# Branch gates through DRAM, attention spread to the end of the gate products, and the written order kept there

## The chip, the core and the metric

The kernel runs on one core of a Trainium2 chip. The core has a matrix engine (PE, with its weight loads shown apart as PEld), a vector engine (DVE), a scalar engine (ACT), a general engine (POOL), and a sync engine (SP) that here only issues transfers. Each engine takes the instructions of its own queue in order, and semaphores make one wait for another. The time is that of one execution on the device in microseconds; a kernel is run several times, and the median counts.

## What is computed

One step of a hybrid layer for 320 tokens, 256 of a new stream and 64 of a running one, model width 2048, all in float32. Cut to what matters:

```python
xn, u, v, q, k, va = _project(xp, norm_mix_g, w_in)        # rmsnorm, one product, gelu on u and v
q, k = _partial_rope(q, pos_p), _partial_rope(k, pos_p)    # 16 of 64 head columns are rotated
vn = _layernorm(v, gmlp_ln_g, gmlp_ln_b)
a = _gmlp_mix(u, vn, gmlp_ws, gmlp_bs)                     # mixes within chunks of 128 tokens
o = _swa_prompt(q, k, va, attn_sinks)                      # 32 heads, 4 key heads, sliding window, sink
g = sigmoid(xn @ w_gate + b_gate); g_a, g_b = halves(g)
x = x + (g_a * (a @ w_branch_a) + g_b * (o @ w_branch_b)) @ w_out
h = _rmsnorm(x, norm_ffn_g)
y = _rmsnorm(x + (silu(h @ w_ffn_gate) * (h @ w_ffn_up)) @ w_ffn_down, final_norm_g)
```

The outputs are y and the new keys, values and normalised v rows.

## The kernel before

**Products.** Activations lie transposed, features on the partitions, tokens on the free axis (T = 320). Each operand is split into a high part `hi` of the type that PE multiplies and the remainder `lo`, and a product takes three matmuls: hi by x-high, hi by x-low, lo by x-high (L168 to L170). A *group* makes 512 output columns: `gemm` (L152) takes four PSUM banks and goes through eight blocks of two row tiles of the weights, 24 matmuls a block, 192 a group. The groups come in the order that `products` lists: first the keys and values (kv, in `first_gemm`), then `QV` (four groups of queries q0 to q3, one for each key head with its eight heads, mixed with four groups of v), then the gates of branch B (gb0 to gb3), w_branch_b (bb), u, the gates of branch A (ga), w_branch_a (ba), w_out and the feed-forward groups.

**Weights.** SP fetches each block of 512 KB into one of four `raw` buffers, four blocks before it is split (`fetch`, L127). ACT writes `hi` (L135) and DVE `lo` (L144), two blocks before their matmuls, into three buffers each. In `gemm`, a block issues `hi` of the block after next, half its matmuls, then `lo` and a fetch, then the rest.

**The calendar.** After every 12 matmuls `gemm` calls `pump()`, which advances a slot counter and issues what `later(slots, fn)` has entered for that slot. There are 16 slots to a group. Small work is hung between the products in this way. Slots are counted here from the end of kv: q0 is slots 1 to 16 and so on to slot 128, the gb groups are slots 129 to 192, bb begins after slot 192.

**Attention.** A group q_g ends in `q_done` (L639): ACT copies the four banks to `qr`; a slot later ACT issues four transfers that bring the partner rows for the rotation to `swp` (`rope_swap`, L365); in slots 5 and 7 after the group `rope_turn` (L370) rotates two tiles each with three DVE operations (times cosine, partner times sine into a scratch tile of the pool tag `st`, sum; L375 to L377). Then ACT and DVE split the queries into high and low (`hi`, `lo` of `q_parts`, L508 and L512), in the five slots before `QK0[g]`. From slot `QK0[g]` after the group, five *units* follow, one for each set of 64 query positions, `5 * n` slots apart (L654). A unit's steps stand in `attend` (L516 to L637), each with its slot: scores on PE (0), peak on DVE (1), exponentials on ACT (2), weights on DVE and ACT (3, 4), pack, a DVE transpose (5), spread, four SP transfers to a DRAM tile `pd` (6), gather, one or two SP transfers back to `pf` (8), part high on ACT (11) and part low on DVE (12), values on PE (14), lower on ACT (15), total on DVE (16). The total puts the unit's output into `f1`. Units of positions 2 to 4 have 192 keys, in a block of 128 and one of 64. 

**v.** A group v_g ends in `v_done` (L659): DVE multiplies by the norm factor, ACT applies the gelu (slot 1), PE transposes (3 to 6), DVE and ACT copy to `tok` (L676, L677), DVE takes statistics (9).

**After QV.** `at = 19` (L748): from 17 slots after the last v group the pool `attn` is closed and the pool `late` opened in its place, the attention's output is split from `f1` into `yh`, `yl` (`split_o`), v is normalised (`v_aggr`, `v_load`, `v_norm`, L728 to L730) and the mixing weights are loaded and turned (`load_ws`, `turn_ws`). This falls into the gb groups. A gb group ends in `sigmoid` (L762): DVE multiplies by the norm factor, ACT applies the sigmoid. The gates of gb0 stay in a tile of tag `st`, those of gb1 to gb3 go to `f1`, whose rows the split has read by then. `flush()` (L778) empties the calendar before bb, and bb multiplies its products with the gates into `f1` (L784).

**Order.** Within `tc.manual_schedule()` each engine gets its instructions as the program writes them. Before, this holds from the start to the end of kv (`startup`, L94 and L487) and for the tail (L941). Between them the tile framework's planner orders the queue of every engine, by its own estimate of durations, from the dependencies and the written order. PSUM has eight banks under one tag: four belong to the current group, the others to scores (two), values, transposes, and to the next group.

Of the kernel before, what the change touches and what calls it, by code (L numbers as in the profile page):

```python
# [10 lines left out]
F32 = mybir.dt.float32  # L11
F32R = mybir.dt.float32r
AF = mybir.ActivationFunctionType
ALU = mybir.AluOpType
# [4 lines left out]
P = 128  # L19
D = 2048  # L20
DC = D // P
T = 320
# [3 lines left out]
W = 512  # L26
# [8 lines left out]
    [(0, 4), (512, 4), (1024, 4), (1536, 4)],  # L35
    [(0, 4), (512, 4), (1024, 4), (1536, 2), (1792, 2)],
]
QV = [("q", 0), ("q", 1), ("v", 0), ("q", 2), ("v", 1), ("q", 3), ("v", 2), ("v", 3)]
QK0 = [14, 24, 18, 12]

NK = [64, 128, 192, 192, 192]
KC = [0, 0, 0, 64, 256]
# [28 lines left out]
def tile_hybrid_step(ctx: ExitStack, tc: tile.TileContext, a: dict, outs: list):  # L71
    nc = tc.nc
    y_p, y_s, ko_p, vo_p, ko_s, vo_s, gv_s = outs
    w_in, w_gate = a["w_in"][0], a["w_gate"][0]
# [5 lines left out]
    tmp = ctx.enter_context(tc.tile_pool(name="tmp", bufs=2))  # L80
    psum = ctx.enter_context(tc.tile_pool(name="psum", bufs=8, space=PSUM))
    dram = ctx.enter_context(tc.tile_pool(name="dram", bufs=1, space=DRAM))
# [8 lines left out]
    def later(slots, fn):  # L91
        calendar.setdefault(now[0] + max(1, slots), []).append(fn)

    startup = tc.manual_schedule()  # L94
    startup.__enter__()

    def pump():
        now[0] += 1
# [3 lines left out]
    def flush():  # L102
        while calendar:
            pump()
# [262 lines left out]
            nc.scalar.dma_start(swp[b : b + 8, 0:nt, :], qr[b + 8 : b + 16, 0:nt, :])  # L367
            nc.scalar.dma_start(swp[b + 8 : b + 16, 0:nt, :], qr[b : b + 8, 0:nt, :])

    def rope_turn(t0):  # L370
        t1 = tmp.tile([P, 2, T], F32, tag="st", name="rope_t1")
        cb = cos_t.unsqueeze(1).broadcast_to([P, 2, T])
        sb = sin_t.unsqueeze(1).broadcast_to([P, 2, T])
        q2 = qr[:, t0 : t0 + 2, :]
        nc.vector.tensor_tensor(q2, q2, cb, op=ALU.mult)  # L375
        nc.vector.tensor_tensor(t1, swp[:, t0 : t0 + 2, :], sb, op=ALU.mult)
        nc.vector.tensor_tensor(q2, q2, t1, op=ALU.add)  # L377

    ka = ap.tile([P, 4, NPOS], F32R, name="ka")
    kl = ap.tile([P, 4, NPOS], F32R, name="kl")  # L380
# [103 lines left out]
        return [p[:, :T] for p in ps]  # L484

    ps = first_gemm()
    startup.__exit__(None, None, None)  # L487
    for t in range(4):
        nc.scalar.activation(qr[:, t, :], ps[t], AF.Copy)
    later(1, lambda: rope_swap(2))  # L490
# [1 line left out]
    for i, n in xs:  # L492
        later(7 + i, lambda i=i, n=n: new_v(i, i * P, n))
        later(9 + 2 * i, lambda i=i: v_blocks(i))
    later(8, lambda: rope_turn(0))
    later(11, k_out)
    later(11, rope_scale)
    for g in range(4):
# [17 lines left out]
    def attend(g, n, qs, st):  # L516
# [72 lines left out]
        def part(low):  # L589
            if not low:  # L590
                st["mm"] = []
            for i, (blk, kn) in enumerate(VB[n]):
                src = st["pf"][:kn, i, :]
                l = vv[:, blk, g, :]
                if kn == P:
                    if not low:
                        st["ph"] = ap.tile([P, 512], F32R, tag="ph", name=f"ph_{g}_{n}")
                        nc.scalar.activation(st["ph"], src, AF.Copy)
                    else:
                        pl = ap.tile([P, 512], F32R, tag="pl", name=f"pl_{g}_{n}")  # L600
                        nc.vector.tensor_tensor(pl, src, f32(st["ph"]), op=ALU.subtract)
                        st["mm"] += [(l, st["ph"]), (l, pl)]
                else:
                    if not low:
                        st["p2"] = ap.tile([P, 512], F32R, tag="p2", name=f"p2_{g}_{n}")
                        nc.scalar.activation(st["p2"][0:64], src, AF.Copy)
                    else:
                        p2 = st["p2"]
                        nc.vector.tensor_tensor(p2[64:128], src, f32(p2[0:64]), op=ALU.subtract)
                        st["mm"] += [(l, p2)]  # L610
# [11 lines left out]
        def total():  # L622
# [9 lines left out]

        return (
            (0, scores), (1, peak), (2, power), (3, lambda: weigh((1, 3))), (4, lambda: weigh((0, 2))),
            (5, pack), (6, spread), (8, gather), (11, lambda: part(False)), (12, lambda: part(True)),
            (14, values), (15, lower), (16, total),
        )  # L637

    def q_done(g, ps):  # L639
        for t in range(4):  # L640
            nc.scalar.activation(qr[:, t, :], ps[t], AF.Copy)
        qs = ap.tile([P, 20, 2, 64], F32R, tag="qs", name=f"qs_{g}")
        hi, lo = q_parts(g, qs)
        later(1, lambda: rope_swap(4))
        later(5, lambda: rope_turn(0))
        later(7, lambda: rope_turn(2))
        at = QK0[g]
        later(at - 5, lambda: hi(0))
        later(at - 4, lambda: lo(0))
        later(at - 3, lambda: hi(1))  # L650
        later(at - 2, lambda: lo(1))
        for n in range(5):
            for dt, step in attend(g, n, qs, {}):
                later(at + 5 * n + dt, step)  # L654


    bst = main.tile([P, 3, 4, 6], F32, name="bst")
# [1 line left out]
    def v_done(g, ps):  # L659
        vst = {}  # L660
        for t in range(4):
            v = tmp.tile([P, T], F32, tag="e1", name=f"v_{g}_{t}", bufs=4)
            nc.vector.tensor_tensor(v, ps[t], rx, op=ALU.mult)

            def curve(v=v):
                nc.scalar.activation(v, v, AF.Gelu_apprx_tanh)

            def turn(t=t, v=v):
                pt = vst[t] = bank(f"vt_{g}_{t}")
                for i, n in xs:  # L670
                    nc.tensor.transpose(pt[:n, i * P : (i + 1) * P], v[:, i * P : i * P + n], ident)

            def put(t=t):
                pt = vst.pop(t)
                c = slice((4 * g + t) * P, (4 * g + t + 1) * P)
                nc.vector.tensor_copy(tok[:, 0:2, c], pt[:, 0:256].rearrange("p (i c) -> p i c", i=2))  # L676
                nc.scalar.activation(tok[0:64, 2, c], pt[0:64, 256:384], AF.Copy)  # L677

            later(1, curve)
            later(3 + t, turn)  # L680
            later(4 + t, put)

        def stats():
            for i, n in xs:
                nc.vector.bn_stats(bst[:n, i, g, :], tok[:n, i, g * W : (g + 1) * W])

        later(9, stats)
# [19 lines left out]
    def split_o(m):  # L707
        for k in range(m, m + 2):
            split(late["yh"][:, k, :], late["yl"][:, k, :], f1[:, k, :])
# [35 lines left out]
        if h == 1:  # L745
            nc.vector.memset(late["wst"][64:128, :, 0:64], 0.0)

    at = 19  # L748
    later(at - 2, open_late)
    for k in range(0, DC, 2):  # L750
        later(at - 2 + k // 2 + 1, lambda k=k: split_o(k))
    later(at + 3, v_aggr)
    for g in range(4):
        later(at + max(1, 9 * g - 2), lambda g=g: v_load(g))
        for i, n in xs:
# [3 lines left out]
    later(at + 40, lambda: turn_ws(0))  # L759
    later(at + 41, lambda: turn_ws(1))  # L760

    def sigmoid(dst, ps, b0, g):  # L762
        for t in range(4):
            m = 4 * g + t
            z = dst(m)
            nc.vector.tensor_tensor(z, ps[t], rx, op=ALU.mult)
            nc.scalar.activation(z, z, AF.Sigmoid, bias=vec[:, b0 + m : b0 + m + 1])

    ps = gemm(w_gate, D, xh, xl, "gb0")
    gate0 = tmp.tile([P, 4, T], F32, tag="st", name="gate0")  # L770

    def gate_b(m):
        return gate0[:, m, :] if m < 4 else f1[:, m, :]

    sigmoid(gate_b, ps, 80, 0)
    for g in range(1, 4):
        sigmoid(gate_b, gemm(w_gate, D + g * W, xh, xl, f"gb{g}"), 80, g)
    flush()  # L778
    yh, yl = late["yh"], late["yl"]
    for g in range(4):  # L780
        ps = gemm(w_bb, g * W, yh, yl, f"bb{g}")
        for t in range(4):
            m = 4 * g + t
            nc.vector.tensor_tensor(f1[:, m, :], ps[t], gate_b(m), op=ALU.mult)  # L784


    wst, bsb = late["wst"], late["bsb"]
# [44 lines left out]
    for g in range(4):  # L832
        ps = gemm(w_ba, g * W, yh, yl, f"ba{g}")
        for t in range(4):
            m = 4 * g + t
# [211 lines left out]
```

## Time and profile before

| | |
|---|---|
| median of three runs | 1952.28 us (1951.65 to 1952.33) |
| the profiled execution | 1951.71 us, its span 1949.8 us |
| instructions in the span | 31855 |
| mean granted clock of PE | 0.997 |
| q0 to q3 and v0 to v3 | 42.35 to 309.69 us |
| gb0 to gb3 | 309.69 to 427.01 us |
| bb0 to bb3 | 427.01 to 539.64 us |

A line of the table by stage gives the stretch in us from the span's start, its length, then for each engine the busy time and the number of instructions, the granted clock of PE as a share of full speed, the mean busy share of the 16 DMA engines, and GB/s. A line of the groups gives line, engine, operation, the tile written and the tiles read, shape and count, then busy us and the mean ns of one, then the idle time of the engine just before these instructions and what ended it. A line of the timeline gives start and duration in us, and in brackets the idle time before it with what released it. In the chain of work that ended last, a DMA piece runs from its issue to its landing.

### The profile page before, as it was taken

The numbers are of one execution on the slowest core, as the hardware profiler recorded it, in microseconds if no ns is written. First come the engines' busy times: TensorE is split into PE (matmuls) and PEld (weight loads), VectorE is DVE, ScalarE is ACT, GpSimd is POOL, SyncE is SP. The second block draws the span as 40 slices with busy tenths as digits, with TensorE's granted clock in tenths as the row PEclk, the third lists the DMA queues.
The fourth block names the chain that finished last, engine by engine and source line by source line (L and its number), as shares of the span: only waits on it lengthen the run. The fifth ranks groups of instructions, "written<-read, shape, count | busy, mean of one in ns | idle before, by whom it ended". The sixth has DMA issues, their size and how long they took to land.

```text
span 1949.8 us, 31855 instructions
## 1 busy us (share of the span) xinstructions
PE 1930.4 (99%) x13207; PEld 1924.3 (99%) x13207; DVE 1042.9 (53%) x1530; ACT 813.4 (42%) x1219; POOL 4.7 (0%) x12
## 2 busy tenths in 40 slices
PE   9999999999999999999999999999999999999997
PEld 9999999999999999999999999999999999999997
DVE  6878887944355544455454444443444444444455
ACT  6666766532233343334443333332333333333343
POOL 0000000000000000000000000000000000000000
PEclk9999999999999999999999999999999999999999
DMA  8566566744444444445445555445555544555443
GB/s 279 158 174 179 163 187 180 223 155 149 149 141 135 146 148 149 149 151 205 151 144 150 151 151 152 152 149 146 150 151 151 152 151 148 146 151 151 152 132 106
DMA packets 171024, 307.41 MB, mean 158 GB/s; under 512 B 11472, under 2 KB 31392, under 8 KB 170688
## 3 DMA queue, kind: packets, MB, share of 16 engines
q1 hardware_dynamic: 166128, 295.67, 49.7%
q10 hardware_dynamic: 4752, 9.72, 1.7%
q8 instruction: 103, 1.69, 0.4%
q14 instruction: 41, 0.34, 0.0%
HBM read 292.15 MB, written 12.45 MB: 156 GB/s over the span
## 4 chain that ended last, share of the span: by engine, by line
PE 92%; DVE 2%; ACT 2%; DMA 2%; issue 1%; SPq 0%; ACTq 0%; DVEq 0%
PE mm_fg L170 5%; PE mm_fd L170 5%; PE mm_fu L170 5%; PE mm_fd L169 5%; PE mm_fu L169 5%; PE mm_fg L169 5%; PE mm_fg L168 5%; PE mm_fu L168 5%; PE mm_fd L168 5%; PE mm_u L168 2%; PE mm_bb L169 2%; PE mm_bb L170 2%; PE mm_ba L168 2%; PE mm_ga L168 2%; PE mm_wo L168 2%; PE mm_wo L169 2%
## 5 line engine op out<-in xcount | busy, mean ns | idle before, releaser
L144 DVE TENSOR_TENSOR lo<-raw,hi 128x1024 fp32r<-128x1024 f32 (+1 forms) x533 | 645.3, 1211 | 660.8 <-ACT hi L135 659.4
L135 ACT ACTIVATE hi<-raw 128x1024 fp32r<-128x1024 f32 (+1 forms) x533 | 559.3, 1050 | 1008.7 <-PE mm_fu L169 188.6
L168 PE MATMUL mm_fd<-xh,hi 128*128 128x320 f32 x704 | 218.2, 310 | 0.0
L168 PE MATMUL mm_fg<-yh,hi 128*128 128x320 f32 x704 | 217.8, 309 | 0.0
L170 PE MATMUL mm_fg<-yh,lo 128*128 128x320 f32 x704 | 217.5, 309 | 0.0
L168 PE MATMUL mm_fu<-yh,hi 128*128 128x320 f32 x704 | 217.5, 309 | 0.0
L169 PE MATMUL mm_fu<-yl,hi 128*128 128x320 f32 x704 | 217.5, 309 | 0.0
L170 PE MATMUL mm_fu<-yh,lo 128*128 128x320 f32 x704 | 217.5, 309 | 0.0
L169 PE MATMUL mm_fg<-yl,hi 128*128 128x320 f32 x704 | 217.5, 309 | 0.0
L170 PE MATMUL mm_fd<-xh,lo 128*128 128x320 f32 x704 | 217.1, 308 | 0.0
L169 PE MATMUL mm_fd<-xl,hi 128*128 128x320 f32 x704 | 217.1, 308 | 0.0
L168 PEld LDWEIGHTS mm_fg<-yh,hi 128*128 128x128 f32 x704 | 132.1, 188 | 0.1
L169 PEld LDWEIGHTS mm_fg<-yl,hi 128*128 128x128 f32 x704 | 132.1, 188 | 0.1
L170 PEld LDWEIGHTS mm_fg<-yh,lo 128*128 128x128 f32 x704 | 132.1, 188 | 0.0
L168 PEld LDWEIGHTS mm_fu<-yh,hi 128*128 128x128 f32 x704 | 132.1, 188 | 0.0
L169 PEld LDWEIGHTS mm_fu<-yl,hi 128*128 128x128 f32 x704 | 132.1, 188 | 0.0
L170 PEld LDWEIGHTS mm_fu<-yh,lo 128*128 128x128 f32 x704 | 132.1, 188 | 0.0
L169 PEld LDWEIGHTS mm_fd<-xl,hi 128*128 128x128 f32 x704 | 132.1, 188 | 0.0
L168 PEld LDWEIGHTS mm_fd<-xh,hi 128*128 128x128 f32 x704 | 132.1, 188 | 0.0
L170 PEld LDWEIGHTS mm_fd<-xh,lo 128*128 128x128 f32 x704 | 132.1, 188 | 0.0
L168 PE MATMUL mm_q<-xh,hi 128*128 128x320 f32 x256 | 81.2, 317 | 0.0
L168 PE MATMUL mm_u<-xh,hi 128*128 128x320 f32 x256 | 80.3, 314 | 0.0
(267 smaller groups left out, 3933.0 us busy)
## 6 DMA issues: line engine op xcount, KB each, us to landing
raw<-in_w_in_dram SPq DMA_DIRECT2D x103, 512.0 KB
raw<-in_w_ffn_gate_dram SPq DMA_DIRECT2D x88, 512.0 KB
raw<-in_w_ffn_up_dram SPq DMA_DIRECT2D x88, 512.0 KB
raw<-in_w_ffn_down_dram SPq DMA_DIRECT2D x82, 512.0 KB
raw<-in_w_gate_dram SPq DMA_DIRECT2D x64, 512.0 KB
raw<-in_w_branch_b_dram SPq DMA_DIRECT2D x32, 512.0 KB
raw<-in_w_branch_a_dram SPq DMA_DIRECT2D x32, 512.0 KB
raw<-in_w_out_dram SPq DMA_DIRECT2D x32, 512.0 KB
```

The costliest lines, as they stand in the source:

```text
L135: nc.scalar.activation(hi[:, :, :n], raws[j][:, :, :n], AF.Copy)
L144: nc.vector.tensor_tensor(lo[:, :, :n], raws.pop(j)[:, :, :n], f32(parts[j][0][:, :, :n]), op=ALU.subtract)
L168: nc.tensor.matmul(o, hi[:, c, cols], xh[:, k, :], start=(k == 0), stop=False)
L169: nc.tensor.matmul(o, hi[:, c, cols], xl[:, k, :], start=False, stop=False)
L170: nc.tensor.matmul(o, lo[:, c, cols], xh[:, k, :], start=False, stop=(k == nk - 1))
```

## The change

It does these things together:

- The written order holds from the start through QV and the gb groups: `startup` becomes `ordered`, left before bb.
- The units of a query group stand seven slots apart (`QKN = 7`), with part low, values, lower and total one slot later in the unit (13, 15, 16, 17). `QV` and `QK0` are new. Units now begin in slots 30, 37, 44, 51, 58 (q0), 66 to 94 (q1), 103 to 131 (q2) and 141 to 169 (q3); the last total stands in slot 186.
- `at = 64`: what followed QV in the gb groups now begins in slot 187 and runs mostly in the bb groups; the splits of `f1` stand 1.5 slots apart.
- The gates of branch B go from a small tile (tag `e1`) to a DRAM tile, one transfer for each output tile on SP; each bb group loads its four back into a tile of tag `st`. `f1` holds only the attention's output until bb.
- The rotation's six operations are one to a slot, from the third slot after the group, cosine products first; the product with the sine is made in place in `swp`, so that the scratch tile goes. For the keys, three operations in slots 8 to 10.
- The larger copy of the transposed v moves from DVE to ACT.
- `flush()` before bb goes.

```diff
-QV = [("q", 0), ("q", 1), ("v", 0), ("q", 2), ("v", 1), ("q", 3), ("v", 2), ("v", 3)]
-QK0 = [14, 24, 18, 12]
+QV = [("q", 0), ("v", 0), ("q", 1), ("v", 1), ("q", 2), ("v", 2), ("v", 3), ("q", 3)]
+QK0 = [14, 18, 23, 13]
+QKN = 7
...
-    startup = tc.manual_schedule()
-    startup.__enter__()
+    ordered = tc.manual_schedule()
+    ordered.__enter__()
...
-    def rope_turn(t0):
-        t1 = tmp.tile([P, 2, T], F32, tag="st", name="rope_t1")
+    def rope_ops(t0):
         cb = cos_t.unsqueeze(1).broadcast_to([P, 2, T])
         sb = sin_t.unsqueeze(1).broadcast_to([P, 2, T])
-        q2 = qr[:, t0 : t0 + 2, :]
-        nc.vector.tensor_tensor(q2, q2, cb, op=ALU.mult)
-        nc.vector.tensor_tensor(t1, swp[:, t0 : t0 + 2, :], sb, op=ALU.mult)
-        nc.vector.tensor_tensor(q2, q2, t1, op=ALU.add)
+        q2, s2 = qr[:, t0 : t0 + 2, :], swp[:, t0 : t0 + 2, :]
+        return (
+            lambda: nc.vector.tensor_tensor(q2, q2, cb, op=ALU.mult),
+            lambda: nc.vector.tensor_tensor(s2, s2, sb, op=ALU.mult),
+            lambda: nc.vector.tensor_tensor(q2, q2, s2, op=ALU.add),
+        )
...
     ps = first_gemm()
-    startup.__exit__(None, None, None)
...
-    later(8, lambda: rope_turn(0))
+    for i, op in enumerate(rope_ops(0)):
+        later(8 + i, op)
...
-            (5, pack), (6, spread), (8, gather), (11, lambda: part(False)), (12, lambda: part(True)),
-            (14, values), (15, lower), (16, total),
+            (5, pack), (6, spread), (8, gather), (11, lambda: part(False)), (13, lambda: part(True)),
+            (15, values), (16, lower), (17, total),
...
         later(1, lambda: rope_swap(4))
-        later(5, lambda: rope_turn(0))
-        later(7, lambda: rope_turn(2))
+        a, b = rope_ops(0), rope_ops(2)
+        for i, op in enumerate((a[0], b[0], a[1], b[1], a[2], b[2])):
+            later(3 + i, op)
...
-                later(at + 5 * n + dt, step)
+                later(at + QKN * n + dt, step)
...
-                nc.vector.tensor_copy(tok[:, 0:2, c], pt[:, 0:256].rearrange("p (i c) -> p i c", i=2))
+                nc.scalar.activation(tok[:, 0:2, c], pt[:, 0:256].rearrange("p (i c) -> p i c", i=2), AF.Copy)
...
-    at = 19
-    later(at - 2, open_late)
+    at = 64
+    later(at - 5, open_late)
     for k in range(0, DC, 2):
-        later(at - 2 + k // 2 + 1, lambda k=k: split_o(k))
-    later(at + 3, v_aggr)
+        later(at - 4 + 3 * k // 4, lambda k=k: split_o(k))
+    later(at + 2, v_aggr)
...
-    def sigmoid(dst, ps, b0, g):
+    def sigmoid(dst, ps, b0, g, done=None):
...
+            if done:
+                done(m, z)
...
-    sigmoid(gate_b, ps, 80, 0)
-    for g in range(1, 4):
-        sigmoid(gate_b, gemm(w_gate, D + g * W, xh, xl, f"gb{g}"), 80, g)
-    flush()
+    gate_d = dram.tile([P, DC, T], F32, name="gate_d")
+    for g in range(4):
+        sigmoid(
+            lambda m: tmp.tile([P, T], F32, tag="e1", name=f"gb_{m}", bufs=4),
+            gemm(w_gate, D + g * W, xh, xl, f"gb{g}"), 80, g,
+            done=lambda m, z: nc.sync.dma_start(gate_d[:, m, :], z),
+        )
+
+    ordered.__exit__(None, None, None)
...
     for g in range(4):
+        gate = tmp.tile([P, 4, T], F32, tag="st", name=f"gate_{g}")
+        nc.sync.dma_start(gate, gate_d[:, 4 * g : 4 * g + 4, :])
         ps = gemm(w_bb, g * W, yh, yl, f"bb{g}")
         for t in range(4):
-            m = 4 * g + t
-            nc.vector.tensor_tensor(f1[:, m, :], ps[t], gate_b(m), op=ALU.mult)
+            nc.vector.tensor_tensor(f1[:, 4 * g + t, :], ps[t], gate[:, t, :], op=ALU.mult)
```

More of the change, by code (lines that the diff above doesn't have):

```diff
@@ L767, in sigmoid @@
             nc.scalar.activation(z, z, AF.Sigmoid, bias=vec[:, b0 + m : b0 + m + 1])
[L769 to L773, printed above, removed]
-    sigmoid(gate_b, ps, 80, 0)
-    for g in range(1, 4):
-        sigmoid(gate_b, gemm(w_gate, D + g * W, xh, xl, f"gb{g}"), 80, g)
-    flush()
+            if done:
[8 more added lines that the diff above has]
+    ordered.__exit__(None, None, None)
     yh, yl = late["yh"], late["yl"]
     for g in range(4):
+        gate = tmp.tile([P, 4, T], F32, tag="st", name=f"gate_{g}")
+        nc.sync.dma_start(gate, gate_d[:, 4 * g : 4 * g + 4, :])
         ps = gemm(w_bb, g * W, yh, yl, f"bb{g}")
         for t in range(4):
-            m = 4 * g + t
-            nc.vector.tensor_tensor(f1[:, m, :], ps[t], gate_b(m), op=ALU.mult)
+            nc.vector.tensor_tensor(f1[:, 4 * g + t, :], ps[t], gate[:, t, :], op=ALU.mult)
     wst, bsb = late["wst"], late["bsb"]
```

## The prediction

> **What bounds the kernel now.** I read the page's first table, then the busy table by stage, then the timeline at the idle stretches, then the groups by line and the chain of waits.
>
> ```profile
> span 1949.8 us, 31855 instructions
> PE 1930.4 (99%) x13207; PEld 1924.3 (99%) x13207; DVE 1042.9 (53%) x1530; ACT 813.4 (42%) x1219; POOL 4.7 (0%) x12
> ```
>
> The matrix engine sets the time, so only its idle time and its slowed time can be won. By stage (stretch, length, busy time of PE, PEld, DVE, ACT, POOL, then granted clock, DMA share, GB/s; the sum covers all nine groups q0 to gb0, of which those with idle time are shown):
>
> ```profile
> ...
> 133.29:170.28 36.99, 34.92 (x241) 34.11 (x240) 31.05 (x60) 28.21 (x71) 0.00 (x0) 1.00 0.62 175
> ...
> 202.48:240.26 37.78, 35.60 (x236) 34.90 (x235) 29.11 (x63) 24.88 (x63) 0.00 (x0) 0.95 0.59 164
> 240.26:274.73 34.47, 33.15 (x225) 32.27 (x224) 30.59 (x53) 22.06 (x50) 0.00 (x0) 1.00 0.67 184
> 274.73:309.69 34.96, 34.63 (x244) 34.00 (x243) 28.29 (x61) 25.68 (x65) 0.00 (x0) 1.00 0.59 170
> 309.69:341.64 31.95, 31.82 (x215) 31.05 (x214) 25.07 (x47) 22.66 (x45) 0.00 (x0) 1.00 0.63 187
> sum 299.29, PE 293.24 PEld 288.66 DVE 243.62 ACT 200.96 POOL 0.00; mean PE 32.58 PEld 32.07 DVE 27.07 ACT 22.33 POOL 0.00
> ```
> ```profile
> 341.64:369.80 28.16, 28.16 (x194) 28.16 (x193) 26.74 (x51) 17.95 (x28) 0.00 (x0) 1.00 0.85 242
> ...
> 427.01:455.16 28.15, 28.15 (x194) 28.15 (x193) 11.49 (x12) 9.49 (x11) 0.00 (x0) 1.00 0.45 150
> ...
> 216.60:220.10 3.50, 3.50 (x16) 3.42 (x15) 3.18 (x7) 3.11 (x8) 0.00 (x0) 0.51 0.30 55
> ```
>
> A group with nothing else on PE takes 28.16 us, 1.76 us for each of its 16 slots. The nine groups idle 299.29 - 293.24 = 6.05 us. The clock stood at 0.51 for 3.50 us: 1.7 us lost. Three of the idle stretches, as the timeline has them:
>
> ```profile
> 146.35 0.55 PE L671 MATMUL vt<-ident,v 128*128 128x128 f32 x3 [2.07 <-ACT pr L546]
> ...
> 215.18 0.50 PE L616 MATMUL o<-ph,vv 128*128 128x512 f32 x1 [2.18 <-ACT pr L546]
> ...
> 261.56 0.47 PE L616 MATMUL o<-p,vv 128*128 128x512 f32 x1 [0.84 <-DVE p L609]
> ```
>
> PE stands because a small step of the attention or of v comes before what it reads is ready; the bracket names what ended the wait. A matmul's record lasts 0.31 us while the next one starts 0.147 us after it (28.16 over 192), so each stretch hides 0.16 us more, 0.8 us over five. What can be won is 6.05 + 0.8 + 1.7 = 8.6 us; the rest of the nine groups is PE's own work, which the change keeps.
>
> **The change, part by part.** Durations:
>
> ```profile
> L144 DVE TENSOR_TENSOR lo<-raw,hi 128x1024 fp32r<-128x1024 f32 (+1 forms) x533 | 645.3, 1211 | 660.8 <-ACT hi L135 659.4
> L135 ACT ACTIVATE hi<-raw 128x1024 fp32r<-128x1024 f32 (+1 forms) x533 | 559.3, 1050 | 1008.7 <-PE mm_fu L169 188.6 <-PE mm_fd L169 184.4 <-PE mm_fg L169 144.6
> ...
> L568 DVE STREAM_TRANSPOSE u<-pr 128x768 f32<-128x768 f32 (+2 forms) x20 | 16.3, 814 | 3.6 <-ACT pr L562 3.5
> ...
> L512 DVE TENSOR_TENSOR qs<-qr,qs 64x1280 fp32r<-64x1280 f32 x8 | 11.9, 1486 | 0.2
> L601 DVE TENSOR_TENSOR pl<-pf,ph 128x512 fp32r<-128x512 f32 x16 | 11.0, 685 | 4.6 <-ACT ph L598 4.5
> L609 DVE TENSOR_TENSOR p<-pf,p 64x512 fp32r<-64x512 f32 x16 | 11.0, 684 | 0.5
> L508 ACT ACTIVATE qs<-qr 64x1280 fp32r<-64x1280 f32 x8 | 10.1, 1268 | 0.4 <-DVE qr L377 0.3
> L730 DVE TENSOR_TENSOR tok<-tok,gb 128x512 f32<-128x512 f32 (+1 forms) x12 | 8.1, 680 | 0.0
> L729 DVE TENSOR_TENSOR tok<-tok,gb 128x512 f32<-128x512 f32 (+1 forms) x12 | 8.1, 679 | 0.0
> L663 DVE TENSOR_TENSOR v<-mm_v,rx 128x320 f32<-128x320 f32 x16 | 7.3, 480 | 0.0
> L377 DVE TENSOR_TENSOR qr<-qr,rope_t 128x640 f32<-128x640 f32 x9 | 7.3, 812 | 0.0
> L676 DVE COPY tok<-vt 128x256 f32<-128x256 f32 x16 | 6.6, 415 | 0.1
> L546 ACT ACT_TABLE_LOAD x5 | 6.4, 1283 | 3.7 <-DVE nm L535 3.7
> L728 DVE TENSOR_SCALAR tok<-tok,mv,rln 128x512 f32<-128x512 f32 (+1 forms) x12 | 6.3, 536 | 0.0
> L767 ACT ACTIVATE gate<-gate,vec 128x320 f32<-128x320 f32 x4 | 1.9, 552 | 0.0
> ```
>
> *Seven slots a unit and a later end.* Attention now ends in slot 186 of the 192 after the key and value product, not in 144. DVE is busy 243.62 of 299.29 us now, 81%; the same work, less the 6.6 us of L676 that go to ACT, runs over the twelve groups, and v_norm (12 x (680 + 679 + 536) ns = 22.7 us) leaves them. This is what should empty the idle stretches: minus 8.6 us, between 0 and 8.6, and I take it whole, since the same waits get two slots (3.5 us) more per unit and the longest was 2.18 us.
>
> *Gates in DRAM.* Sixteen writes of 160 KB and four loads of 640 KB join SP's queue. A write waits for its sigmoid, at most 4 x 0.55 + 1.28 + 0.5 = 4 us after a group's end, and the fetch of raw weights behind it waits too; a fetch is four blocks (14 us) ahead of its use, so I cost this at nothing. If that cover went, 4 us at each of four ends. A load is issued 28 us ahead of its use, beside a DMA share of 0.45.
>
> *Late work into the w_bb groups.* The 22.7 us of v_norm and the smaller pieces fall where DVE is busy 11.49 of 28.15 us a group: hidden. The eight transposes of turn_ws move along: zero.
>
> *Table loads.* Sigmoids (after slots 144 and 160) now stand between exponentials, which makes four more loads of 1.283 us on ACT: 5.1 us, beside ACT's 17.95 of 28.16 us: hidden. [...]
>
> *Order of the groups, buffers.* The q and v groups change places; they are the same eight products. The rotation's scratch tile goes, since the sine product is made in place: nothing on the path.
>
> *Rotation, one operation to a slot.* The first operation stands three slots after the q group (5.28 us); it used to stand four slots after the swap, and only its release by the swap counts:
>
> ```profile
> 173.00 0.42 ACT L641 ACTIVATE qr<-mm_q 128x320 f32<-128x320 f32 x1
> ...
> 179.63 0.82 DVE L375 TENSOR_TENSOR qr<-qr,cos_t 128x640 f32<-128x640 f32 x1 [0.36 <-DMA swp<-qr]
> ...
> 242.12 0.44 ACT L641 ACTIVATE qr<-mm_q 128x320 f32<-128x320 f32 x1
> ...
> 249.51 0.82 DVE L375 TENSOR_TENSOR qr<-qr,cos_t 128x640 f32<-128x640 f32 x1 [0.30 <-DMA swp<-qr]
> ```
>
> The swap released it 9.35 and 9.25 us after the groups' ends (170.28, 240.26). ACT's copies ended 3.1 and 2.3 us after those ends, the release came 6.2 and 6.95 us after the copies; with copies on time (four of 0.44, 1.8 us) it comes 8.2 us after the end at the earliest. In written order DVE is therefore held 2.9 to 4.0 us at its slot, and behind it stand the weights' lo, the peaks, the packs and the low halves (pl, p) of other units. After q1 and q2 the query split stands 13 and 18 slots behind the group, and DVE can catch up. After q3 (slot 128) it stands in slot 136, the same as the last rotation, and PE's values of an older unit in slot 139. Between them, in queue order: last rotation 0.81, query split 1.27, hi 1.05, lo 1.21, pl and p 1.37 = 5.71 us against three slots, 5.28. PE waits 0.4 us if DVE comes on time. DVE comes late by the hold and six rotations (4.9 us), less what is free in five slots (8.8 us): lo takes 1.21 of 3.52 us, 34%; the other 47% of today's 81% shrinks to five sevenths, 33%; a third is free, 2.9 us. So the wait reaches 0.4 + 2.9 + 4.9 - 2.9 = 5.3 us with copies on time and 6.4 with copies as late as now. Between 0.4 and 5.3 I take the middle, 2.9 us, and keep 0.4 and 6.4 as bounds. The other narrow place is slot 66: values need a PSUM bank that v1's first product gives up, behind pl, p, the query's lo and that product on DVE (1.37 + 1.49 + 0.48 = 3.34 us against two slots, 3.52). Of q1's group, 13 slots back, DVE has the hold (2.9), six rotations (4.9) and the first lo (1.49) to make up, in a third of 22.9 us, 7.6: late by 1.7, a wait of 1.5 us at most. I take 0 there: the free third is a low estimate, as it counts every other DVE step at its full rate, and keep 1.5 as its bound.
>
> *Clock.* Of two stretches of equal size (2.07 and 2.18 us) one was followed by the half clock. A wait of 2.9 us would be a like case, so I charge half of 1.7: 0.85 us. [...]
>
> Sum: -8.6 + 2.9 + 0.85 = -4.85 us. The profiled execution took 1951.71 us, 1.9 beyond its span and 0.6 below the median of 1952.28; against its own time that gives 1946.9, against the median **1947.4 us**.
>
> **Rivals.** *Clean* (chance 0.11): DVE's fewer busy hours absorb the held rotation, nothing new waits over 1 us: 1952.3 - 8.6 + 0.8 = 1944.5. For it: every later stage runs at 28.16 us with no idle. Against it: the swap's 9.3 us are measured.
>
> *Given back* (0.34): both narrow places near their bounds, 1.5 + 4.7, with the half clock, 1.7: 7.9 us, and 1951.6. For it: DVE and ACT pass lateness on, since hi and lo stand in the same queues.
>
> *The round trip decides* (0.20, slower). The probabilities go through DRAM between pack and part:
>
> ```profile
> 122.10 3.61 DMA pd<-u
> ...
> 125.72 3.66 DMA pf<-pd
> ```
> ```profile
> 300.62 4.84 DMA pd<-u
> ...
> 305.90 2.89 DMA pf<-pd
> ```
> ```profile
> L577 SPq DMA_DIRECT2D pd<-u x80: 312/441/1804, 109.8 to 324.8; - x80
> ```
>
> Pack 0.81, three issues of 0.44, 4.84 + 2.89 (or 3.61 + 3.66) to land, 0.4 of issue: 9.8 to 10.3 us against the six slots, 10.56, that stand between them before and after the change. A pack that is late by 0.5 us holds ACT at part, hi behind it, then lo and the next pack, so lateness is carried from unit to unit once it passes that point, and the two slots between part's low half and values are used up. With 12 units of two key blocks at 1.1 us each, half of the longest stretch now, 13.2 us: 1952.3 - 8.6 + 13.2 = 1956.9. Against it: four DMA issues in a row, instead of fetches between them, shorten the way.
>
> **How the numbers follow.** Forecast 0.35, clean 0.11, given back 0.34, round trip 0.20. A change of 0.2% (3.9 us) is about what a measurement of this kernel can tell from none: faster by more takes forecast and clean, 0.46; within it given back, 0.34; slower the round trip, 0.20. The range runs from all 8.6 us and 0.9 more of PE's small steps, 1942.8, to just past the round trip's price, 1957.5; the forecast's own range, by the bounds 0.4 and 6.4 with the clock at 0 and 1.7, is 1944.1 to 1951.8.
>
> **What would show it.** Right: the groups q0 to gb3 take 384.7 us now (42.35 to 427.01) and some 380 then; no idle before vt L671; the first rotation of a q group released by the swap, with a hold of 2 to 4 us on DVE; one idle stretch of about 3 us before values in the group after q3; the w_bb groups at 28.2 us plus the moved 0.9. Wrong: the chain of waits names pd and pf at most units (round trip), raw weights after gate writes, or bb's first block waits for the split of the attention's output.

## The result, and the profile after

The changed kernel takes 1964.38 us (median of four runs, 1963.57 to 1966.07), the kernel before 1951.97 us (four runs beside them). The ratio is 1.0066, with a 95% interval of 1.0052 to 1.008: 12.4 us slower, and outside the range of the prediction, 1942.8 to 1957.5.

The first lines of the page of the changed kernel:

```profile
span 1963.1 us, 31858 instructions
PE 1935.6 (99%) x13207; PEld 1926.1 (98%) x13207; DVE 1037.8 (53%) x1514; ACT 821.4 (42%) x1238; POOL 4.7 (0%) x12
```

The span grew by 13.3 us, PE's busy time by 5.2 only. The busy table by stage, columns as before: the two worst groups, q2 and gb0, and the sum from q0 to gb3, the stretch that was to shrink from 384.7 to some 380 us.

```profile
168.87:207.57 38.70, 35.33 (x237) 34.80 (x235) 26.27 (x46) 25.76 (x58) 0.00 (x0) 0.96 0.50 142
...
306.98:346.01 39.03, 33.80 (x216) 32.37 (x215) 27.06 (x44) 20.95 (x44) 0.00 (x0) 0.96 0.57 160
...
sum 396.99, PE 382.35 PEld 374.59 DVE 279.04 ACT 246.10 POOL 0.00; mean PE 31.86 PEld 31.22 DVE 23.25 ACT 20.51 POOL 0.00
```

The stretch is 396.99 us, 12.3 longer than before; PE stands idle for 14.64 us of it. The same stretch of the kernel before:

```profile
42.35:427.01 384.66, 378.61 (x2591) 374.01 (x2589) 306.50 (x563) 240.06 (x509) 0.00 (x0) 1.00 0.62 180
```

DVE was busy for 306.50 us there and is for 279.04 now: it has less to do, as forecast, and PE waits for it all the same. The span grew by 1.0 us more than the stretch: 0.9 of it are the transposes of `turn_ws`, which moved to the w_bb groups. PE has no idle time there (first and third group):

```profile
439.49:467.64 28.15, 28.15 (x194) 28.15 (x193) 24.87 (x43) 11.79 (x14) 0.00 (x0) 1.00 0.69 222
...
495.80:524.82 29.02, 29.02 (x202) 29.01 (x201) 13.27 (x15) 8.49 (x8) 0.00 (x0) 1.00 0.56 186
```

The waits of the changed kernel from 42 to 440 us, engine by engine (who waits for what: us in all, times, longest):

```profile
PE o L618 <- DVE pl L603: 7.2, 4, 4.4
PE o L618 <- DVE v L666: 3.4, 1, 3.4
PE o L618 <- DVE p L611: 1.7, 6, 0.3
PE pk L427 <- DVE qr L378: 1.2, 1, 1.2
PE mm_v L171 <- DVE lo L145: 0.7, 1, 0.7
...
DVE lo L145 <- ACT hi L136: 92.6, 54, 4.9
...
ACT ph L600 <- DMA pf<-pd: 21.8, 10, 4.8
```

And of the kernel before, in the same stretch:

```profile
PE vt L671 <- ACT pr L546: 2.4, 2, 2.1
PE o L616 <- ACT pr L546: 2.2, 1, 2.2
...
DVE lo L144 <- ACT hi L135: 47.0, 39, 3.0
...
ACT ph L598 <- DMA pf<-pd: 9.5, 5, 4.2
```

PE's old waits, for ACT, are gone; PE waits for DVE now. And DVE itself stands 92.6 us at the weights' `lo` for `hi`, against 47.0. The longest wait, in slot 139, as the timeline has it (lines of other work left out; the group gb0 starts at 306.98):

```profile
312.89 1.23 DVE L145 TENSOR_TENSOR lo<-raw,hi 128x1024 fp32r<-128x1024 f32 x1 [4.54 <-ACT hi L136]
...
318.91 0.83 DVE L376 TENSOR_TENSOR qr<-qr,cos_t 128x640 f32<-128x640 f32 x1 [1.36 <-DMA pd<-u]
...
324.38 0.63 ACT L600 ACTIVATE ph<-pf 128x512 fp32r<-128x512 f32 x1 [0.71 <-DMA pf<-pd]
...
328.83 0.78 DVE L378 TENSOR_TENSOR qr<-qr,swp 128x640 f32<-128x640 f32 x1
...
329.65 1.27 ACT L510 ACTIVATE qs<-qr 64x1280 fp32r<-64x1280 f32 x1 [3.42 <-DVE qr L378]
330.82 1.04 ACT L136 ACTIVATE hi<-raw 128x1024 fp32r<-128x1024 f32 x1
...
331.89 1.22 DVE L145 TENSOR_TENSOR lo<-raw,hi 128x1024 fp32r<-128x1024 f32 x1 [2.28 <-ACT hi L136]
333.04 0.68 DVE L603 TENSOR_TENSOR pl<-pf,ph 128x512 fp32r<-128x512 f32 x1
...
333.77 0.50 PE L618 MATMUL o<-pl,vv 128*128 128x512 f32 x1 [4.39 <-DVE pl L603]
```

Read it from the end. `pl` had its operands at 325.0, when `ph` was done, and starts 8.0 us later. For 2.28 of these 8.0 us DVE stands idle at `lo`, which is ahead of `pl` in its queue; the rest goes to the other steps written ahead of `pl`, which were late themselves. DVE had lost 4.54 us at the `lo` of an earlier block, whose `hi` came after ACT had waited 3.42 us at part for a gather, and 1.36 us at the first rotation (first two lines). `lo` waits for `hi`; `hi` stands in ACT's queue behind the query's high part, which held ACT for 3.42 us until DVE's last rotation. So DVE waits for ACT, which waited for DVE, with ready work behind both, and PE pays. DVE's queue is taken in written order in these rows: DVE idles for 2.28 us at `lo` with a `pl` behind it that needs nothing more.

### The profile page after: what moved, and what is told of

Read it like the earlier page. It is cut to its first block, busy times and chain, and to the rows that moved or that the text cites. A ratio compares the mean times of both kernels' runs of the same rounds, so it can differ in the third digit from the quotient of the medians.

```text
span 1963.1 us, 31858 instructions
## 1 busy us (share of the span) xinstructions
PE 1935.6 (99%) x13207; PEld 1926.1 (98%) x13207; DVE 1037.8 (53%) x1514; ACT 821.4 (42%) x1238; POOL 4.7 (0%) x12
## 4 chain that ended last, share of the span: by engine, by line
PE 92%; DVE 3%; ACT 2%; DMA 1%; issue 1%; SPq 0%; ACTq 0%; DVEq 0%
PE mm_fd L169 5%; PE mm_fu L170 5%; PE mm_fd L170 5%; PE mm_fg L170 5%; PE mm_fu L169 5%; PE mm_fg L169 5%; PE mm_fg L171 5%; PE mm_fu L171 5%; PE mm_fd L171 5%; PE mm_u L169 2%; PE mm_ba L171 2%; PE mm_ba L169 2%; PE mm_bb L170 2%; PE mm_wo L171 2%; PE mm_ga L169 2%; PE mm_ga L171 2%
```

## The experiments

Eighteen kernels were run; ratios are against the kernel before, run beside each (its medians in the five sessions were 1950.8 to 1951.7 us). The expectations number the theories: 1, narrow places in the calendar; 2, the way of the probabilities through DRAM; 3, the written order itself; 4 and 5, the holds at `lo` and at part. A letter marks a variant. They count PE's waits from matmul to matmul, with what the records hide: 3.5 us in slot 66 and 5.4 in slot 139, where the rows above say 3.4 and 4.39 and 0.31.

| run | median us | ratio, 95% interval |
|---|---|---|
| planner | 1944.53 | 0.9967 (0.9955 to 0.998) |
| before_written | 1972.50 | 1.0104 (1.0089 to 1.0119) |
| old_rotation | 1960.57 | 1.0049 (1.0034 to 1.0064) |
| q3_early | 1960.61 | 1.0051 (1.0036 to 1.0066) |
| split_shift | 1963.71 | 1.0063 (1.0048 to 1.0078) |
| wide_split | 1965.50 | 1.0068 (1.0055 to 1.0082) |
| values_late | 1971.32 | 1.0101 (1.0084 to 1.0118) |
| no_trip | 1963.21 | 1.0063 (1.0048 to 1.0078) |
| part_free | 1959.48 | 1.0039 (1.0024 to 1.0054) |
| part_12 | 1957.39 | 1.0034 (1.0022 to 1.0046) |
| lo_late | 1949.56 | 0.9992 (0.9982 to 1.0001) |
| lo_late_part_12 | 1948.03 | 0.9982 (0.9973 to 0.9992) |
| lo_late_part_free | 1948.50 | 0.9984 (0.9974 to 0.9993) |
| planner_oldrot | 1944.89 | 0.9968 (0.9956 to 0.9981) |
| planner_5 | 1947.39 | 0.9981 (0.9972 to 0.999) |
| planner_q3 | 1945.69 | 0.9971 (0.9961 to 0.9982) |
| written_from_q1 | 1943.70 | 0.9961 (0.9948 to 0.9973) |
| planner_lo_late | 1942.70 | 0.9956 (0.9943 to 0.997) |

**The order alone, in the new places and in the old ones.** The run planner:

```diff
     ps = first_gemm()
+    ordered.__exit__(None, None, None)
...
-    ordered.__exit__(None, None, None)
     yh, yl = late["yh"], late["yl"]
```

> The changed kernel with the written order left after the key and value product, as in the kernel before; slots, order of groups, gates in DRAM as changed. Theory 3 (written order is the loss): the planner moves what is ready ahead of what waits, and the twelve groups come to the time of the kernel before or less: 1945 to 1952 us. Theories 1 and 2 (the slots of the steps, the length of the round trip): the data are as late as before, the planner wins back only what queued behind them: 1956 to 1962 us.

The run before_written:

```diff
-    startup.__exit__(None, None, None)
...
-        nc.vector.tensor_tensor(t1, swp[:, t0 : t0 + 2, :], sb, op=ALU.mult)
-        nc.vector.tensor_tensor(q2, q2, t1, op=ALU.add)
+        s2 = swp[:, t0 : t0 + 2, :]
+        nc.vector.tensor_tensor(s2, s2, sb, op=ALU.mult)
+        nc.vector.tensor_tensor(q2, q2, s2, op=ALU.add)
...
     flush()
+    startup.__exit__(None, None, None)
```

> The kernel before (its slots, order of groups and gates), with the written order kept to the end of the gate products; the rotation's sine product is made in place, since its scratch tile would block DVE in written order. Theory 3a (written order costs its 20 us in any layout, 1964.4 against 1944.5 in the new one): 1966 to 1976 us. Theory 3b (the old places suit the written order, only the new ones do not): 1951 to 1956 us.

The two runs complete a square. In the old places the planner gives 1951.7 us and the written order 1972.5; in the new places 1944.5 and 1964.4. The written order costs 20.8 and 19.9 us, the new places gain some 7 to 8 us: two effects that hardly touch each other. (before_written differs from the kernel before in one more thing, the sine product in place.) In the new places PE's idle time makes 13.5 of the 19.9 us (14.64 against 1.12 in the stretch) and its half clock 3.4. The planner's run, by stage and by waits:

```profile
42.52:418.86 376.34, 375.22 (x2583) 371.93 (x2581) 280.26 (x503) 252.00 (x529) 0.00 (x0) 1.00 0.62 186
```
```profile
PE vt L675 <- ACT pr L549: 1.0, 1, 1.0
...
DVE lo L145 <- ACT hi L136: 43.5, 37, 3.0
```

With the same slots, PE has one wait left and DVE's hold at `lo` is back at 43.5 us. The same place as above in the planner's timeline, gb0 starting at 296.00:

```profile
311.72 1.06 ACT L136 ACTIVATE hi<-raw 128x1024 fp32r<-128x1024 f32 x1 [0.71 <-PE mm_gb L170]
...
313.94 1.22 DVE L145 TENSOR_TENSOR lo<-raw,hi 128x1024 fp32r<-128x1024 f32 x1
314.05 2.57 ACT L511 ACTIVATE qs<-qr 64x1280 fp32r<-64x1280 f32 x2 [1.27 <-DVE qr L378]
315.07 0.69 DVE L604 TENSOR_TENSOR pl<-pf,ph 128x512 fp32r<-128x512 f32 x1
```

`hi` now stands ahead of the query's high part, `lo` finds it done, and `pl` comes 19.1 us after the group's start; in written order it was 26.1.

**Single places: rotation, splits, values.** Each edit takes away what seemed to hold one place. old_rotation:

```diff
-        for i, op in enumerate((a[0], b[0], a[1], b[1], a[2], b[2])):
-            later(3 + i, op)
+        for i, op in enumerate(a):
+            later(5, op)
+        for i, op in enumerate(b):
+            later(7, op)
...
-        later(8 + i, op)
+        later(8, op)
```

> The changed kernel with the rotation placed as in the kernel before: three operations together at slots 5 and 7 behind a q group, and all three at slot 8 behind the key and value group (the sine product stays in place). Changed kernel: 1964.4 us; its waits ahead of values in slots 66 and 139 are 3.5 and 5.4 us, each followed by half clock (1.7 us), and the key transposes wait 1.4 us. Theory 1 (narrow places: the one-operation rotation puts the query split and what stands behind it late): both waits shrink by the slot that the last rotation comes earlier (1.76 us) and by what the swap no longer holds, and the 1.4 us go: 1955 to 1960 us. Theory 2 (round trip through DRAM holds ScalarE at part): only the 1.4 us of the keys go: 1963 us. Theory 3 (written order itself is the loss): likewise 1963 us.

q3_early:

```diff
-QV = [("q", 0), ("v", 0), ("q", 1), ("v", 1), ("q", 2), ("v", 2), ("v", 3), ("q", 3)]
-QK0 = [14, 18, 23, 13]
+QV = [("q", 0), ("v", 0), ("q", 1), ("v", 1), ("q", 2), ("v", 2), ("q", 3), ("v", 3)]
+QK0 = [14, 18, 23, 29]
```

> The changed kernel with q3's group ahead of v3's, and the query split of q3 at its old slots (136 to 139), now 24 slots behind its group in place of 8. Theory 1: the wait of 5.4 us in slot 139 and the 1.7 us of half clock behind it go, nothing else moves: 1957.3 us. Theory 2: the wait stays, since ScalarE is held at part by the gather all the same: 1962 to 1964 us. Theory 3: 1962 to 1964 us.

split_shift:

```diff
-QK0 = [14, 18, 23, 13]
+QK0 = [14, 17, 23, 14]
...
-    at = 64
+    at = 65
```

> The changed kernel with the split of q1 and its units one slot earlier, and the split of q3, its units and the work behind them one slot later: hi(0) of q3 then stands in a slot at whose end the weights' hi is queued already. Theory 1b (weights' hi stands behind the query's hi in ScalarE's queue, which waits for the last rotation, and so lo, pl and p wait for the split): the wait in slot 139 falls from 5.4 us to about 2 and the half clock behind it goes, the wait in slot 66 falls from 3.5 by 1.8 us: 1956 to 1959 us. Rival (the rotation itself is late, the split's place doesn't matter): 1962 to 1964 us.

wide_split:

```diff
-QK0 = [14, 18, 23, 13]
+QK0 = [14, 20, 25, 16]
...
-    at = 64
+    at = 67
```

> The changed kernel, in written order, with the splits of q1, q2 and q3 and their units 2, 2 and 3 slots later, and the work behind attention 3 slots later; nothing else is moved. Theory 1c (written order costs its 20 us at the few places where a query split stands close behind its rotation): the waits in slots 66 and 139 and their half clock, 12.3 us, go: 1952 us. Rival (any place will do: an in-order queue hands each wait on to the next): new waits elsewhere, 1958 to 1966 us.

values_late:

```diff
-            (15, values), (16, lower), (17, total),
+            (18, values), (19, lower), (20, total),
...
-    at = 64
+    at = 67
```

> The changed kernel with values, lower and total three slots (5.3 us) later in each unit, and the work behind attention three slots later. Theory 3d (in written order PE reaches values before DVE has made pl and p, where the planner puts values behind more matmuls): every wait at values goes, 14 us, and the two stretches of half clock, 3.4 us: 1947 us, with only the keys' 1.4 us and the 1.2 us at the weights of v0 left. Rival (lateness is only handed on, since the next unit's ph and p wait for the later values): 1958 to 1964 us.

The first two win 3.8 us each, about half of what theory 1 gave q3_early and less than it gave old_rotation; the next two win nothing that can be told, and values_late loses 7. PE's waits in split_shift and in wide_split, and in values_late those of PE and ACT, show why:

```profile
PE s L526 <- DVE qs L514: 4.7, 1, 4.7
PE o L618 <- DVE pl L603: 2.5, 3, 1.8
```
```profile
PE o L618 <- DVE pl L603: 7.1, 4, 2.8
PE o L618 <- DVE v L666: 3.5, 1, 3.5
```
```profile
PE s L526 <- DVE qs L514: 8.2, 2, 4.7
...
ACT ph L600 <- PE o L618: 13.0, 5, 9.6
```

In split_shift the later split of q3 takes the wait in slot 139 from 4.4 to 1.8 us, as theory 1b had it, but the split of q1, one slot earlier, makes the scores in slot 65 wait for it, 4.7 us. Splits two and three slots later leave the waits at `pl` at 7.1 us in all, in other slots; values three slots later hold ACT, up to 9.6 us, at the next unit's `ph`, whose buffer they free. A wait at one place goes, and the lateness comes out at another. Theory 1 falls as the whole cause: 12.3 us were to go in wide_split, and none went.

**The way through DRAM.** no_trip, part_free and part_12:

```diff
-            rows = st["d"].rearrange("k c b x -> (k c) (b x)")
+            rows = w_in[0:192, 0:512]
```

> The changed kernel with the gather reading rows of the weight matrix in place of the unit's probabilities: all transfers are there, but the gather and part no longer wait for the spread (leaves out that the values see the probabilities). Theory 2 (round trip): all waits at pl and p go, some 10 us with the clock: 1954 us. Theory 1: the waits in slots 66 and 139 come from the rotation and the query split and stay; only the four small waits at pl and p in other slots (0.8, 2.5, 1.0, 1.8 us) go: 1958 to 1961 us. Theory 3: part of each, 1958 to 1962 us.

```diff
-                src = st["pf"][:kn, i, :]
+                src = f32(xh).rearrange("p k t -> p (k t)")[:kn, 512 * i : 512 * i + 512]
```

> The changed kernel with part reading rows of x in SBUF in place of the gathered probabilities; all transfers are still made (leaves out that the values see the probabilities). ScalarE waits 21.8 us at part for the gather in the changed kernel. Theory 2b (this hold of ScalarE is what makes hi, lo, packs and the low halves late): 1950 to 1956 us, and DVE's wait at lo falls from 92.6 us towards the 43.5 of the planner's order. Theory 3c (each queue's own order of hi, lo, rotation and split is the cause): 1960 to 1963 us, waits in slots 66 and 139 stay over 2 us.

```diff
-(11, lambda: part(False)), (13, lambda: part(True)),
+(12, lambda: part(False)), (13, lambda: part(True)),
```

> The changed kernel, in written order, with the high half of part one slot (1.76 us) later, the rest of the unit in place. Theory 5 (ScalarE's hold at part): with the gathered probabilities free of any wait the time was 1959.5 us; of the 21.8 us of hold in ten places up to 1.76 us each go: 1960 to 1962 us. Rival (pl and p, a slot behind, then come later): 1964 to 1967 us.

A gather that needs no spread wins 1.2 us, less than these measurements tell apart. It isn't free of the unit's pace either: it stands behind the spread in SP's queue. ACT still waits for it:

```profile
ACT ph L600 <- DMA pf<-in_w_in_dram: 15.8, 8, 5.3
```

Where part waits for no transfer at all, 4.9 us go, and DVE's hold at `lo` stays:

```profile
DVE lo L145 <- ACT hi L136: 93.4, 60, 4.6
```

One slot more ahead of part wins 7.0 us, more than was expected; the intervals of the two overlap. So the gather's lateness has a price of about 5 to 7 us in this order, but it isn't what holds DVE.

**DVE's hold at lo.** lo_late writes each block's `lo`, and the weight fetch behind it, a slot later, so that DVE's queue doesn't come to it before ACT has had time for `hi` (`in_order` is true from the start to the end of the gate products). The next two add the edits above to it.

```diff
-                if t == 1:
+                if t == (3 if in_order[0] else 1):
                     if todo:
                         low(ahead)
                     fetch(ahead + RAWS)
```

> The changed kernel, in written order, with each block's lo (and the fetch behind it) written one slot later, so that ScalarE has two slots for hi before DVE's queue stands at lo; a block's lo is then ready a whole block ahead of its use still. Theory 4 (DVE's hold at lo is how the written order loses its 20 us): the wait at lo falls from 92.6 to about 45 us and the time to 1948 to 1954 us. Rival (the hold only stands where DVE would have been idle, or moves to the matrix engine's weights): 1960 to 1968 us.

> Both edits together. If DVE's hold at lo and ScalarE's hold at part are separate losses, the two gains add up: 1945 to 1951 us. If one is the cause of the other: no better than the better of the two alone.

> Lo one slot later and part reading rows of x in place of the gathered probabilities (leaves out that the values see the probabilities). If these two holds are all that the written order loses: the planner's 1944.5 us, within 2. If a third is behind it (the rotation's hold, values before their bank is free): 1949 to 1957 us.

One slot for `lo` wins 14.8 of the 19.9 us. The waits of lo_late:

```profile
PE mm_v L172 <- DVE lo L146: 2.4, 3, 1.4
PE pk L428 <- DVE qr L379: 1.7, 1, 1.7
...
DVE lo L146 <- ACT hi L137: 34.0, 33, 2.8
...
ACT ph L601 <- DMA pf<-pd: 11.0, 8, 2.4
```

The hold at `lo` is 34.0 us in place of 92.6. The waits in slots 66 and 139, at the splits and at the other values, all go but 0.5 us, though nothing was done there; and ACT's hold at part halves. Could the later fetch have done that, since spread and gather stand behind it in SP's queue? The traces speak against it: from a pack's end to the issue of its gather it is 6.2 us in the mean of the 20 units in both kernels. What changed is the packs: by the timelines of PE and DVE they start 2.8 us on average behind the matmul that they are written after in the changed kernel, and 0.4 us in lo_late. So most of the hold at part was a consequence of late packs, which stood behind `lo`. The later slot for part adds 1.5 us here by the medians, not 7.0; the part that waits for nothing adds 1.1. The intervals overlap with that of lo_late alone. The gains of the two edits don't add up, as is to be expected if one hold passes on the other. What lo_late_part_12 still waits for lies in the first two groups alone: 1.7 us ahead of the key transposes, 2.3 at v0's weights.

**Which of the new places gain, and the best of both.** In the planner's order, one edit each on planner: `QKN = 5`; the rotation of old_rotation; the lists of q3_early.

> The planner's order from the end of the key and value product on, as in the run of 1944.5 us, with five slots a unit in place of seven; each q group's first unit stays in its slot. If the seven slots make the gain, as the prediction had it: 1949 to 1952 us. If the later end and the order of the groups are enough: 1944 to 1946 us.

> The planner's order from the end of the key and value product on, as in the run of 1944.5 us, with the rotation placed as in the kernel before (three operations together). If the one-operation rotation has no part in the 7 us that the new places bring under the planner: 1943.5 to 1945.5 us. If it has: 1946 to 1950 us.

> The planner's order from the end of the key and value product on, as in the run of 1944.5 us, with q3's group ahead of v3's. The planner's run has one wait left, 1.2 us ahead of v1's transposes, which this does not touch: 1944 to 1945 us. If the place of q3's split, 8 slots behind its group, still cost something under the planner: 1942 to 1943.5 us; if v3's curve and transposes then fall among the gates' sigmoids and exponentials: 1946 us.

Five slots give back 2.9 of the 6.7 us. The rotation's place changes the time by 0.4 us, nothing that can be told. q3 ahead of v3 is 1.2 us worse by the medians, with intervals that overlap, as was expected if v3's transposes come among the gates: PE waits 1.4 us for them in gb0. The last two runs take both edits, lo a slot later and the high half of part in slot 12, into the planner's order (planner_lo_late) or into the written order from q1 on (written_from_q1):

```diff
     for c, g in QV:
+        if (c, g) == ("q", 1):
+            ordered = tc.manual_schedule()
+            ordered.__enter__()
+            in_order[0] = True
```

> Lo one slot later and the high half of part one slot later, with the planner's order in q0's and v0's groups and the written order from q1 to the end of the gate products. If the 4.7 us of waits left in written order (1.9 ahead of the key transposes, 2.8 at v0's weights) are the order's cost in these two groups: 1943.3 us, 1 us below the planner alone. If the steps that wait there are late whatever the order: 1946 to 1948 us.

> The planner's order from the end of the key and value product on, with both edits. If the planner sets hi and lo by readiness whatever the place they are written in: 1944 to 1945 us, as without the edits. If it keeps to the written place where two are ready: up to 1.2 us less, the one wait that it has left.

Both come out below both kernels. The stretch q0 to gb3 in written_from_q1, and in planner_lo_late:

```profile
42.63:418.71 376.08, 375.62 (x2582) 371.94 (x2581) 279.56 (x499) 246.45 (x524) 0.00 (x0) 1.00 0.61 187
```
```profile
42.33:417.16 374.83, 374.83 (x2582) 372.00 (x2581) 279.08 (x503) 251.31 (x529) 0.00 (x0) 1.00 0.61 186
```

In the second PE is busy for 374.83 of 374.83 us: no idle time is left there that order or place could win. The waits left in lo_late_part_12 (4.0 us by the rows, 4.7 with what the records hide) were the order's cost in q0's and v0's groups: they are gone in written_from_q1 (1943.7 measured, 1943.3 expected). The planner gains from the two edits too, 1.8 us by the medians and 1.4 by the distance from the kernel before beside each; the intervals overlap, but the one wait that it had, 1.0 us, is gone from the trace.

## Why the prediction was wrong, point by point

- **What can be won, 8.6 us, and its place: right.** Under the planner the new places gain 6.7 us, with both edits 8.1 (1950.8 to 1942.7), and PE's idle time goes from 6.05 us to none. In written order they gain about as much, 8.1 by the medians. Of the old waits for ACT one of 1.0 us is left in the planner's run.
- **Why they gain: half shown.** "The same waits get two slots (3.5 us) more per unit" holds for 2.9 of the 6.7 us (planner_5). The rest lies with the other new places, which were not taken one by one, save that the rotation brings nothing and q3's place 1.2 us at most.
- **The step that failed: the sum prices the written order at the rotation alone.** The prediction wrote "In written order DVE is therefore held 2.9 to 4.0 us at its slot" and worked DVE's whole lateness out from that hold: 2.9 us, and 0.85 for the clock. That hold measured 1.54, 1.56, none and 1.36 us after the four q groups, less than forecast. The hold of DVE at `lo`, 92.6 us in the stretch, has no term in the sum. The written order costs 20 us in either set of places, and in the new places 14.8 of it go when each block's `lo` stands a slot later, so that DVE's queue doesn't reach it so far ahead of ACT's `hi`. The row that gave this away was quoted: L144 idle for 659.4 us of the whole span, waiting for `hi`. It was read as a duration only. In the planner's order such a wait, 43.5 us in the stretch, costs PE next to nothing (PE idles 1.12 us there); in written order, with 92.6 us, ready steps stand behind it.
- **Narrow place in slot 139:** the wait is there, 4.39 + 0.31 us, within 0.4 and 6.4 but above the 2.9 taken. Its cause is not the one that was worked out: DVE came late by 4.54 and 2.28 us at `lo` and 1.36 at the rotation. In wide_split, with the split three slots later, 0.3 us is left of it, and others appear.
- **Narrow place in slot 66:** taken at 0 with a bound of 1.5, measured 3.4. The steps are those that the prediction named, in its order: pl and p, the query's lo, v1's product. What made them late is again the hold at `lo`, 2.69 and 0.94 us in the two blocks before:

```profile
164.90 1.23 DVE L145 TENSOR_TENSOR lo<-raw,hi 128x1024 fp32r<-128x1024 f32 x1 [2.69 <-ACT hi L136]
...
170.33 1.23 DVE L145 TENSOR_TENSOR lo<-raw,hi 128x1024 fp32r<-128x1024 f32 x1 [0.94 <-ACT hi L136]
...
173.77 1.49 DVE L514 TENSOR_TENSOR qs<-qr,qs 64x1280 fp32r<-64x1280 f32 x1
175.28 1.68 DVE L666 TENSOR_TENSOR v<-mm_v,rx 128x320 f32<-128x320 f32 x4
```

  With the split two slots later the wait stays at 3.5 us (wide_split), where the first half of the query's lo stands in the place of the second; with the weights' `lo` a slot later it is gone, though the query's lo still stands there.
- **Clock:** 0.85 charged. Two waits, 3.4 and 4.4 us, were each followed by half clock, 1.7 us each.

```profile
177.32:180.72 3.40, 3.40 (x15) 3.40 (x15) 2.98 (x7) 2.04 (x4) 0.00 (x0) 0.50 0.34 88
334.33:337.73 3.40, 3.15 (x11) 3.08 (x12) 3.34 (x4) 0.60 (x1) 0.00 (x0) 0.50 0.94 256
```

- **Not foreseen:** the keys' rotation, spread over slots 8 to 10 against transposes in slot 11, 1.2 us.
- **Gates in DRAM, table loads, late work, order of groups at nothing: right.** In lo_late_part_12, which has them all, PE waits nowhere after v0. Three table loads were added (5, 4 and 3 before; 7, 4 and 4 now), not four.
- **Rivals.** "The round trip decides" had the sign and, at 1956.9, the nearest time, and lateness is handed on from unit to unit as it said. But the trip isn't the source: without its wait 1.2 us go, without any gather 4.9, and ACT's hold at part halves when `lo` is moved. "Given back" named the mechanism, lateness that DVE and ACT pass on because `hi` and `lo` stand in the same queues (DVE's 92.6 us at `lo`), but priced it at the two narrow places, 7.9 us, and came out at 1951.6. "Clean" gave 1944.5, which is what the planner's order makes of the same slots; that the numbers meet is chance, since "Clean" was meant for the written order.

## What to carry to other kernels

Before writing out an order by hand, list which engine stands idle in front of which instruction in the planned order, and ask what would stand behind it: an idle time that costs next to nothing there, as DVE's 43.5 us at `lo` did here, can become a hold on ready work, here 92.6 us. Where two engines make the halves of one split, try a slot more between the first and the second half; here it was worth 14.8 us. When moving a step takes a wait away at one place and brings one of the same size at another, stop moving steps and look for the hold that all of them stand behind.

## What the runs showed that was not expected

Cut at its ends, the half clock between 42 and 440 us lasts 3.4 us each of the two times in the changed kernel, as above, and 3.41 us the one time in the kernel before; a stretch in old_rotation is twice as long, 6.82 us:

```profile
216.63:220.04 3.41, 3.41 (x15) 3.33 (x15) 3.09 (x7) 3.02 (x8) 0.00 (x0) 0.50 0.30 53
```
```profile
175.44:182.26 6.82, 6.82 (x28) 6.57 (x28) 4.39 (x10) 5.45 (x17) 0.00 (x0) 0.50 0.58 175
```

In the kernel before it followed a wait of PE of 2.18 us, while one of 2.07 us was not followed by it. In the changed kernel it followed waits of 3.4 and 4.39 us, and not one of 1.78 us (at `pl`, ended at 253.04). What decides is not shown. In planner, lo_late, lo_late_part_12, written_from_q1 and planner_lo_late the longest wait of PE between 42 and 440 us is 1.7 us (lo_late), and the mean granted clock of their executions is 0.997 or 0.998, against 0.994 or 0.995 in the changed kernel.
